# MLP up-projection as a 2x2 block product in seven products, with smaller blocks and the down-projections between the pairs

## Chip, cores and metric

One core of a Trainium2 chip runs the kernel in one launch. The metric is the device time in microseconds (us), the median of several runs of the same kernel.

## What is computed

One layer of a hybrid backbone for 640 tokens (512 latent, 128 context, `T = 640`) with a model width of 1024. The change touches only the gated MLP at the layer's end:

```python
h2 = rms_norm(x, n2) * (1 + sc2) + sh2
u_val, u_gate = jnp.split(dw_conv(h2 @ w_up, f_conv), 2, axis=-1)
x = x + gt2 * ((jax.nn.silu(u_gate) * u_val) @ w_dn)
```

`w_up` is 1024 x 5632 (2816 value columns, then 2816 gate columns), `w_dn` is 2816 x 1024, and `dw_conv` is a width-3 convolution along the tokens, done apart for the latent and the context tokens. Everything is float32.

## The kernel before, in words

Activations lie transposed in SBUF: 128 channels on the partitions, 640 tokens along a row. So `h2` is eight tiles of 128 channels (`KT = 8`), and the 2816 MLP channels are 22 tiles (`NF = 22`), each with a value tile (`uv`) and a gate tile (`ug`).

Each float32 product is made of three products in a shorter format (float32r). Every operand is split into a high part (a rounding cast on ScalarE) and a low part (the rest, a subtraction on VectorE), and TensorE sums high x high, low x high and high x low. For weights `w_split` does this (lines L142 and L143) from a staging buffer `raw` that `w_load` (L135) fills by a DMA on SP's queue. The `ring` holds three `raw` buffers and two each of `wh` and `wl`. `plan` is the list of all weight tiles in the order of use. `W(key)` takes the next one, and issues the load two entries ahead and the split one entry ahead, at a higher priority than the code around it.

`gemm_b` (L297) runs one tile of weights, 8 tiles deep for an up, over the 640 tokens in two halves of 320 (`HALF`): 8 x 3 x 2 = 48 matmuls of 320 columns. Its result stands in a `gtile` of two PSUM banks, and the pool `psg` has two such tiles, used in turn. A gemm can start only when the gemm before the last has been read out.

The MLP runs in four blocks of 6, 6, 5 and 5 channel tiles (`FBLK`). `ffn_up(b)` makes the value and gate tile of each channel tile, then `conv` (L438 on ScalarE, four operations of L440 on VectorE), SiLU (L1579), the product of the two (L1580), and a split into the high and low `ac` tiles (L330, L331). `ffn_down(b)` runs eight downs, one for each output tile `nt`, over the block's `ac` tiles (36 or 30 matmuls), and adds each to `x1[nt]` with two VectorE operations (L1589), one for the 512 latent columns and one for the 128 context columns. `ffn_up(b + 1)` stands ahead of `ffn_down(b)`. The first gemms of block 0 (`up_early`) start before the norm's scale is known.

The framework's scheduler takes the code and its priorities and sets the order in which each engine gets its instructions; that order is then fixed, and every engine runs its own strictly in turn.

Of the kernel before, what the change touches and what calls it, by code (L numbers as in the profile page):

```python
# [58 lines left out]
def hybrid_step(ctx: ExitStack, tc: tile.TileContext, a: dict, o: list):  # L59
# [27 lines left out]
    def body(ps):  # L87
        return ps[:, OFF:OFF + T]
# [110 lines left out]
    for nt in range(8):  # L199
        plan_cols(("wo", nt), w_out, nt * P)  # L200
    FBLK = [6, 6, 5, 5]
    fst = [0, 6, 12, 17]

    def plan_up(b):
        for f in range(fst[b], fst[b] + FBLK[b]):
            plan_cols(("uv", f), w_up, f * P)
            plan_cols(("ug", f), w_up, DFF + f * P)

    def plan_down(b):
        for nt in range(8):  # L210
            plan_cols(("wd", b, nt), w_dn_, nt * P, FBLK[b], P, fst[b])

    plan_up(0)
    for b in range(4):
        if b < 3:
            plan_up(b + 1)
        plan_down(b)

    pidx = {g[0]: i for i, g in enumerate(plan)}
    loaded, split = {}, {}  # L220
    LOOK_L, LOOK_S = 2, 1
    used = [0]

    def W(key):
        i = pidx[key]
        assert i == used[0], (key, i, used[0])
        used[0] += 1
        with tc.high_priority() if i else nullcontext():
            for j in range(i, min(i + LOOK_L + 1, len(plan))):
                if j not in loaded:  # L230
                    loaded[j] = w_load(*plan[j][1:])
                if j <= i + LOOK_S and j not in split:
                    split[j] = w_split(loaded[j], *plan[j][2:])
        return split[i]
# [1248 lines left out]
    gx = {}  # L1483

    def actile():
        return ep.tile([P, T + 2], F32R, tag="ac", bufs=24, name=nm("ac"))

    for nt in range(8):
        ps = gtile()
        if nt < 7:  # L1490
            x_load(nt + 1)
        gemm_b(ps, W(("wo", nt)), lambda k: mgH[:, k, :], lambda k: mgL[:, k, :], KT)
        x1[nt] = x()
        tr_chunks(xns.pop(nt).rearrange("p c x -> p (c x)"),
                  lambda c0, n, v, nt=nt: S.copy(x1[nt][:, c0 * P:(c0 + n) * P], v.rearrange("p c x -> p (c x)")))
# [3 lines left out]
        g, gh, gl = gx[nt] = [actile() for _ in range(3)]  # L1499
        for r, (c0, c1) in enumerate(((0, TS), (TS, T))):  # L1500
            S.activation(out=g[:, c0:c1].bitcast(F32), in_=x1[nt][:, c0:c1], func=AF.Copy, scale=A2[:, nt, r:r + 1])
        V.tensor_copy(g[:, T:].bitcast(F32), modc[:, 24 + nt, :])
        split_x(g.bitcast(F32), gh, gl)
        if nt == 0:
            S.activation(out=sacc, in_=x1[nt], func=AF.Square)
        else:
            sq = ep.tile([P, T], F32, tag="sq", bufs=2, name=nm("sq"))
            S.activation(out=sq, in_=x1[nt], func=AF.Square)
            (V if nt == 7 else G).tensor_tensor(out=sacc, in0=sacc, in1=sq, op=ALU.add)

    early = {}
# [25 lines left out]
    dg = ep.tile([P, T], F32, name="dg")
    rst = ep.tile([P, T], F32, name="rst")
    for c0, n in ((0, 4), (4, 1)):
# [3 lines left out]
        PE.matmul(out=pb[:, :n * P], lhsT=ones, rhs=dg[:, c0 * P:(c0 + n) * P], start=True, stop=True)  # L1543
        V.tensor_copy(rst[:, c0 * P:(c0 + n) * P], pb[:, :n * P])
    for _ in ug0:
        pass
    up_scale("uv", 0)
    up_scale("ug", 0)
    for _ in up_early("uv", 1):
        pass  # L1550
    h2H = actp.tile([P, KT, T], F32R, tag="aH", name="h2H")
    h2L = actp.tile([P, KT, T], F32R, tag="aL", name="h2L")
    for k in range(KT):
        g = gx[k][0][:, :T].bitcast(F32)
# [11 lines left out]
    def ffn_up(b, order):
        for f in order:
            ys = {}

            for key, f2 in sorted((("uv", f), ("ug", NF + f)), key=lambda i: (i[0], f) in early):  # L1570
                y = ys[key] = ep.tile([P, T], F32, tag="fy", bufs=4, name=nm("fy"))
                if (key, f) in early:
                    src = early[key, f]
                else:
                    ps = gtile()
                    gemm_b(ps, W((key, f)), lambda k: h2H[:, k, :], lambda k: h2L[:, k, :], KT)
                    src = body(ps)
                conv(y, src, lambda tap, f2=f2: fcols[:, tap, f2:f2 + 1])
            S.activation(out=ys["ug"], in_=ys["ug"], func=AF.Silu)  # L1579
            V.tensor_mul(ys["uv"], ys["uv"], ys["ug"])  # L1580
            ac[f] = [actile()[:, :T] for _ in range(2)]
            split_x(ys["uv"], *ac[f])

    def ffn_down(b):
        for nt in range(8):
            ps = gtile()
            gemm_b(ps, W(("wd", b, nt)), lambda k: ac[fst[b] + k][0], lambda k: ac[fst[b] + k][1], FBLK[b])
            for r, (c0, c1) in enumerate(((0, TS), (TS, T))):
                V.scalar_tensor_tensor(out=x1[nt][:, c0:c1], in0=body(ps)[:, c0:c1], scalar=modc[:, 40 + nt, r:r + 1],  # L1589
                                       in1=x1[nt][:, c0:c1], op0=ALU.mult, op1=ALU.add)  # L1590
            if b == 3:
                yt = ep.tile([P, NCH, P], F32, tag="xn", bufs=2, name=nm("yt"))
                tr_chunks(x1[nt], lambda c0, n, v: S.copy(yt[:, c0:c0 + n, :], v))
                ns_ = slice(nt * P, (nt + 1) * P)
                SY.dma_start(out=y_s[0, :, ns_].rearrange("(c p) d -> p c d", p=P), in_=yt[:, 0:4, :])
                SY.dma_start(out=y_p[0, :, ns_], in_=yt[:, 4, :])
# [40 lines left out]
```

## Time and profile before

| | us |
|---|---|
| median of 3 runs | 1397.82 (1394.4 to 1398.26) |
| profiled execution, its own time | 1397.2 |
| its span, first to last instruction | 1395.4 |

The profile comes from the profiled execution, which is 0.6 us below the median and has 1.8 us outside its span. In it TensorE is busy 96% of the span, VectorE 56%, ScalarE 38% and GpSimd 12%. The MLP takes about the last third: the chain of work that ended last shows one unbroken piece of TensorE work from 953.5 to 1355.4 us, and then the last eight downs with their transposes and stores.

### The profile page before, as it was taken

The page shows a single profiled execution, that of the slowest core. Times are in us where ns is not written, and L with a number is a line of the kernel's source. Part 1 is how long each engine was busy: PE and PEld are TensorE (multiplying, and loading weights), DVE is VectorE, ACT ScalarE, POOL GpSimd, SP SyncE. Part 2 cuts the span into 40 slices and gives each one's busy share as a digit, 9 for nine tenths or more (in the row PEclk, how much of TensorE's full clock was granted, in tenths as well). Part 3 has the DMA queues.
Part 4 walks back from the last instruction along what each step waited for, and adds up shares of the span by engine and source line. Part 5 has one row for each costly group of instructions (what it writes and reads, how often), then busy time and mean ns, then how long its engine had stood idle before and what let it go on. Part 6 is the DMA issues. An engine that isn't in the chain of part 4 may idle for free.

```text
span 1395.4 us, 26764 instructions
## 1 busy us (share of the span) xinstructions
PE 1339.1 (96%) x11201; PEld 1273.1 (91%) x11201; DVE 777.4 (56%) x1629; ACT 523.5 (38%) x968; POOL 168.2 (12%) x188
## 2 busy tenths in 40 slices
PE   5999999998989899999999998998999999999998
PEld 4899999898878798999998898998999999999998
DVE  3675876775788753334343335567555445535532
ACT  4543334422575432333333424554333223213312
POOL 1011122202223310102120022100000000000000
PEclk9999999998989999999999999999999999999999
DMA  9623331222012153434344534322222232132123
GB/s 273 169 61 86 98 78 41 56 76 64 24 32 55 40 105 94 111 94 112 102 120 144 149 89 140 99 76 61 76 76 65 73 91 69 58 97 70 54 85 86
DMA packets 198731, 123.79 MB, mean 89 GB/s; under 512 B 20341, under 2 KB 192147, under 8 KB 198611
## 3 DMA queue, kind: packets, MB, share of 16 engines
q1 hardware_dynamic: 198227, 121.76, 31.9%
q8 instruction: 88, 1.44, 0.4%
q10 hardware_dynamic: 384, 0.33, 0.1%
q14 instruction: 32, 0.26, 0.1%
HBM read 115.51 MB, written 6.55 MB: 87 GB/s over the span
## 4 chain that ended last, share of the span: by engine, by line
PE 74%; DVE 6%; ACT 4%; POOL 3%; issue 2%; DMA 0%; SPq 0%; ACTq 0%; DVEq 0%; POOLq 0%
PE g L297 60%; PE g L318 2%; PE s L545 1%; PE s L345 1%; PE s L1371 1%; DVE wl L143 1%; PE s L1359 1%; POOL ssn L267 1%; PE m L1321 1%; DVE stmp L903 1%; DVE Y L905 1%; POOL xa L1233 1%; POOL xb L1233 1%; PE m L1023 1%; PE m L715 1%
## 5 line engine op out<-in xcount | busy, mean ns | idle before, releaser
L142 ACT CAST wh<-raw 128x1024 fp32r<-128x1024 f32 (+3 forms) x172 | 161.4, 939 | 472.5 <-PE g L297 386.5
L143 DVE TENSOR_TENSOR wl<-raw,wh 128x1024 fp32r<-128x1024 f32 (+3 forms) x172 | 187.5, 1091 | 235.5 <-ACT wh L142 223.8
L297 PE MATMUL g<-hH,wh 128*128 128x320 f32 x768 | 187.2, 323 | 3.2 <-DVE xb L653 1.6
L297 PE MATMUL g<-hL,wh 128*128 128x320 f32 x768 | 183.4, 318 | 0.6 <-DVE hL L393 0.6
L297 PE MATMUL g<-hH,wl 128*128 128x320 f32 x768 | 183.5, 317 | 0.0
L297 PE MATMUL g<-h2H,wh 128*128 128x320 f32 x656 | 150.5, 311 | 4.0 <-DVE fy L440 4.0
L297 PE MATMUL g<-ac,wh 128*128 128x320 f32 (+1 forms) x800 | 151.7, 310 | 0.0
L297 PE MATMUL g<-h2L,wh 128*128 128x320 f32 x656 | 150.6, 311 | 0.0
L297 PE MATMUL g<-h2H,wl 128*128 128x320 f32 x656 | 150.4, 311 | 0.0
L297 PEld LDWEIGHTS g<-hH,wh 128*128 128x128 f32 x768 | 129.5, 191 | 11.8 <-issue 4.3
L297 PEld LDWEIGHTS g<-hL,wh 128*128 128x128 f32 x768 | 130.9, 192 | 3.3 <-issue 1.8
L297 PEld LDWEIGHTS g<-hH,wl 128*128 128x128 f32 x768 | 131.4, 192 | 2.3 <-issue 1.9
L297 PEld LDWEIGHTS g<-ac,wh 128*128 128x128 f32 x800 | 125.5, 188 | 0.2 <-issue 0.2
L297 PEld LDWEIGHTS g<-h2H,wh 128*128 128x128 f32 x656 | 110.7, 189 | 4.3 <-issue 4.3
L297 PEld LDWEIGHTS g<-h2H,wl 128*128 128x128 f32 x656 | 110.5, 189 | 0.0
L297 PEld LDWEIGHTS g<-h2L,wh 128*128 128x128 f32 x656 | 110.5, 189 | 0.0
L318 PE MATMUL g<-wh,hH 128*128 128x256 f32 x320 | 95.2, 297 | 3.4 <-DVE xb L653 3.4
L318 PE MATMUL g<-wl,hH 128*128 128x256 f32 x320 | 94.9, 297 | 0.0
L318 PE MATMUL g<-wh,hL 128*128 128x256 f32 x320 | 94.5, 295 | 0.0
L297 PE MATMUL g<-ac,wl 128*128 128x320 f32 (+1 forms) x400 | 91.7, 310 | 0.0
L440 DVE SCALAR_TENSOR_TENSOR fy<-g,fcols,fy 128x127 f32<-128x127 f32 (+1 forms) x164 | 86.1, 546 | 2.6
L1589 DVE SCALAR_TENSOR_TENSOR xa<-g,modc,xa 128x512 f32<-128x512 f32 x64 | 34.5, 548 | 89.2 <-PE g L297 89.2
(551 smaller groups left out, 2271.2 us busy)
## 6 DMA issues: line engine op xcount, KB each, us to landing
raw<-in_w_in_dram SPq DMA_DIRECT2D x64, 512.0 KB
raw<-in_w_up_dram SPq DMA_DIRECT2D x44, 512.0 KB
wada<-in_w_ada_dram SPq DMA_DIRECT2D x32, 512.0 KB
wat<-in_w_ada_dram SPq DMA_DIRECT2D x16, 512.0 KB
raw<-in_w_branch_dram SPq DMA_DIRECT2D x24, 256.0 KB
raw<-in_w_down_dram SPq DMA_DIRECT2D x16, 384.0 KB
raw<-in_w_down_dram SPq DMA_DIRECT2D x16, 320.0 KB
raw<-in_w_out_dram SPq DMA_DIRECT2D x8, 512.0 KB
```

The costliest lines, as they stand in the source:

```text
L142: S.copy(wh[:, :m], raw[:, :m])
L143: V.tensor_sub(wl[:, :m], raw[:, :m], wh[:, :m].bitcast(F32))
L267: G.tensor_tensor(out=out, in0=out, in1=mh.broadcast_to([P, n]), op=ALU.pow)
L297: PE.matmul(out=ps[:, OFF + c0:OFF + c1], lhsT=ww[:, k, :], rhs=xx(k)[:, c0:c1], start=(k == 0 and i == 0), stop=(k == kt - 1 and i == 2))
L318: PE.matmul(out=ps[b][:, o:o + GRP], lhsT=xx[:, 4 * kh + k, cs], rhs=ww[:, k, :], start=(kh == 0 and c % 2 == 0 and k == 0 and i == 0), st ...
L345: PE.matmul(out=pa[32 * g:32 * g + 32, :w], lhsT=csil[:, k, :], rhs=t[g], start=start, stop=stop)
L440: V.scalar_tensor_tensor(out=y[:, o0:o1], in0=src[:, i0:i0 + o1 - o0], scalar=w3(t), in1=y[:, o0:o1], op0=ALU.mult, op1=ALU.add)
L545: PE.transpose(pt[:, i * P:(i + 1) * P], src[:, (c0 + i) * P:(c0 + i + 1) * P], ident)
L715: PE.matmul(out=pv[b * w:(b + 1) * w, c, :], lhsT=K[r, c * P + b * w:c * P + (b + 1) * w], rhs=Q[r, c * P + qb * w:c * P + (qb + 1) * w], ...
L903: V.tensor_tensor(out=tv, in0=Uw[w, 0:k, k:k + 1].broadcast_to([64 + NB, k, m]), in1=Y[w, k:k + 1, k + 1:32].broadcast_to([64 + NB, k, m]) ...
L1233: G.tensor_tensor(out=out, in0=acc, in1=t, op=ALU.add)
L1589: V.scalar_tensor_tensor(out=x1[nt][:, c0:c1], in0=body(ps)[:, c0:c1], scalar=modc[:, 40 + nt, r:r + 1], in1=x1[nt][:, c0:c1], op0=ALU.mul ...
```

## The change

Blocks 1 to 5 are new: 22 tiles stand in six blocks of 4, 4, 4, 4, 3 and 3. Block 0 is made as before. From tile 4 on (18 tiles), `up_pair(f)` makes the value and the gate tile at once. Weights and activations are read as 2x2 matrices: the rows are value and gate, the inner index is the two halves of the 1024 channels (`kh`), the columns are the two token halves L and R. Seven products of 12 matmuls (4 channel tiles, three products each) take the place of eight (84 matmuls for a pair, 96 before). Four of the left factors and four of the right are sums or differences of blocks.

- Weights: four `plan` entries for a pair, named q0 to q3 here. `st_load` fetches the blocks. For q1 and q2 a second DMA on GpSimd's queue adds a block of `w_up` to what the first has landed (L250, `accum_op`). `st_sums` makes two more sums on VectorE (L258, L260). q0 to q2 are 1024 wide, q3 is 512.
- Activations: `sums_h2` makes, once, four sums and differences of `h2` for each of four channel tiles and splits them into the `hs` tiles.
- Results: X and Y are the two banks of one `gtile`, Z is an `stile` (one bank). X, Y and Z are each read between two products and added to again, so `up_pair` copies or combines parts in SBUF (`u1`, `u2`): two copies on ScalarE (L1689, L1699), five 320-column operations on VectorE. `conv` then reads `u1` and `u2` from SBUF.
- Downs: those of block b - 1 follow the pairs of block b, two after each pair (2, 3 and 3 in the blocks of three). There are 48 instead of 32, over 4 or 3 tiles (24 or 18 matmuls). Their weights have their own buffers (`rawd`, `whd`, `wld`, two each).

```diff
+    def st_load(f, j):
+        raw = st_raw[f, j] = ring.tile([P, 1024], F32, tag="raw", bufs=RAWB, name=nm("raw"))
...
+        SY.dma_start(out=lo, in_=part(*((0, 0), (1, 0), (0, 0), (1, 1))[j]))
+        if j in (1, 2):
+            G.dma_start(out=lo, in_=part(1, 2 - j), accum_op=ALU.add)
+        if j == 1:
+            SY.dma_start(out=hi, in_=part(0, 1))
+        return raw
+
+    def st_sums(f, j):
+
+        if j == 0:
+            V.tensor_add(st_raw[f, 0][:, 512:], st_raw[f, 0][:, :512], st_raw[f, 1][:, :512])
+        elif j == 2:
+            V.tensor_add(st_raw[f, 2][:, 512:], st_raw[f, 0][:, 512:], st_raw[f, 1][:, 512:])
...
+    def up_pair(f):
+
+        ps = gtile()
+        X, Y, Z = ps[:, :HALF], ps[:, 512:512 + HALF], stile()[:, :HALF]
...
+        w = W(("st", f, 0))
+        prod(X, w, 0, lambda j, k: hH2[j][:, k, L], True, False)
+        with tc.high_priority():
+            S.copy(u2[:, L], X)
+        prod(Y, w, 1, lambda j, k: hs[k, 1][j][:, R], True, False)
+        with tc.high_priority():
+            V.tensor_sub(u1[:, R], u2[:, L], Y)
+        w = W(("st", f, 1))
+        prod(Z, w, 0, lambda j, k: hs[k, 0][j][:, L], True, False)
+        with tc.high_priority():
+            V.tensor_add(u2[:, R], u2[:, L], Z)
+        prod(X, w, 1, lambda j, k: hH2[j][:, 4 + k, L], False, True)
+        with tc.high_priority():
+            S.copy(u1[:, L], X)
+        w = W(("st", f, 2))
+        prod(Y, w, 0, lambda j, k: hs[k, 0][j][:, R], False, False)
+        with tc.high_priority():
+            V.tensor_sub(u2[:, R], Y, u2[:, R])
+        prod(Z, w, 1, lambda j, k: hH2[j][:, 4 + k, R], False, True)
+        with tc.high_priority():
+            V.tensor_add(u1[:, R], u1[:, R], Z)
+        w = W(("st", f, 3))
+        prod(Y, w, 0, lambda j, k: hs[k, 1][j][:, L], False, True)
+        with tc.high_priority():
+            V.tensor_sub(u2[:, L], Y, u2[:, L])
...
-    ffn_up(0, (1, 2, 0, 3, 4, 5))
-    for b in range(4):
-        if b < 3:
-            ffn_up(b + 1, range(fst[b + 1], fst[b + 1] + FBLK[b + 1]))
-        ffn_down(b)
+    up_tile(1)
+    up_tile(2)
+    sums_h2(0)
+    sums_h2(1)
+    up_tile(0)
+    up_tile(3)
+    sums_h2(2)
+    sums_h2(3)
...
+    for b in range(1, NB_F):
+        for i in range(FBLK[b]):
+            up_pair(fst[b] + i)
+            for nt in downs(b, i):
+                down(b - 1, nt)
+    for nt in range(8):
+        down(NB_F - 1, nt)
```

How the scheduler then orders the instructions shows at three places. The first is TensorE at the start of a gemm that needs a PSUM tile. Before, at a down in the middle of a block (`g` is the down's PSUM tile, `ac` the gated activations, `wh` and `wl` its split weights; what an instruction waits for stands in brackets):

```order
L297 MATMUL g_1537_12821<-ac_1439_11772,wh_1534_12777 128x320 x2
L297 MATMUL g_1537_12821<-ac_1440_11773,wh_1534_12777 128x320 x2
L297 MATMUL g_1537_12821<-ac_1439_11772,wl_1535_12778 128x320 x2
L297 MATMUL g_1541_12866<-ac_1379_11132,wh_1538_12822 128x320 [waits DVE_49,PE_49,Activation_49]
L297 MATMUL g_1541_12866<-ac_1379_11132,wh_1538_12822 128x320
```

Now, at the start of a pair in the middle of a block (`s` is Z, `g` is X and Y, `r` are the `hs` tiles):

```order
L1681 MATMUL s_1442_12211<-r12_9538,wh_1444_12215 128x320
L1681 MATMUL s_1442_12211<-r13_9539,wh_1444_12215 128x320
L1681 MATMUL s_1442_12211<-r12_9538,wl_1445_12216 128x320
L1681 MATMUL g_1441_12210<-h2H_10355,wh_1439_12180 128x320 [waits DVE_49,PE_49]
L1681 MATMUL g_1441_12210<-h2L_10356,wh_1439_12180 128x320
L1681 MATMUL g_1441_12210<-h2H_10355,wl_1440_12181 128x320
```

Z's first product now stands ahead of X, and X waits for a VectorE instruction: the second addition (128 columns) of the first of the two downs ahead, whose PSUM tile X takes over. From X on the order in a pair is X (12 matmuls), 6 of a down, Y (12), 5 of that down, X again (12), 7 of Z, Y (12), 5 of Z, Y (12), the last 13 of that down, 24 of the second down, and the next pair's Z (12).

The second place is VectorE over the downs behind a pair. Before (`xa` is `x1[nt]`):

```order
L1589 SCALAR_TENSOR_TENSOR xa7_489<-g_1537_12821,modc_252,xa7_489 128x512
L143 TENSOR_TENSOR wl_1543_12868<-raw_1540_12826,wh_1542_12867 128x768
L1589 SCALAR_TENSOR_TENSOR xa7_489<-g_1537_12821,modc_252,xa7_489 128x128
L1589 SCALAR_TENSOR_TENSOR xa6_488<-g_1541_12866,modc_252,xa6_488 128x512
L143 TENSOR_TENSOR wl_1547_12913<-raw_1544_12871,wh_1546_12912 128x768
```

Now, the last 12 rows up to the addition for which X above waits (`t` are `u1`, `u2` and the convolution's results; ahead of these rows stand the last combination of the pair, L1710, then L260, one L489 of 511 columns and one L150 of 1024):

```order
L150 TENSOR_TENSOR wld_1454_12313<-rawd_1449_12278,whd_1453_12312 128x512
L150 TENSOR_TENSOR wl_1445_12216<-raw_1438_12175,wh_1444_12215 128x1024
L489 SCALAR_TENSOR_TENSOR t0_9519<-t2_9521,fcols_242,t0_9519 128x511
L489 SCALAR_TENSOR_TENSOR t0_9519<-t2_9521,fcols_242,t0_9519 128x127
L489 SCALAR_TENSOR_TENSOR t4_9523<-t3_9522,fcols_242,t4_9523 128x511
L150 TENSOR_TENSOR wld_1458_12347<-rawd_1452_12310,whd_1457_12346 128x512
L489 SCALAR_TENSOR_TENSOR t0_9519<-t2_9521,fcols_242,t0_9519 128x127
L489 SCALAR_TENSOR_TENSOR t4_9523<-t3_9522,fcols_242,t4_9523 128x511
L489 SCALAR_TENSOR_TENSOR t4_9523<-t3_9522,fcols_242,t4_9523 128x127
L1722 SCALAR_TENSOR_TENSOR xa5_487<-g_1433_12141,modc_252,xa5_487 128x512
L489 SCALAR_TENSOR_TENSOR t4_9523<-t3_9522,fcols_242,t4_9523 128x127
L1722 SCALAR_TENSOR_TENSOR xa5_487<-g_1433_12141,modc_252,xa5_487 128x128
```

A down's additions stood by themselves, with one weight split between them; now both convolutions and four weight splits of the pair stand ahead of them.

The third place is GpSimd's queue in the MLP. Before, its last rows were the sums of squares and one small power (`rs2`), and nothing came behind them:

```order
L1509 TENSOR_TENSOR sacc_9519<-sacc_9519,sq_1244_9838 128x640 [waits Activation_49,Pool_49]
L1509 TENSOR_TENSOR sacc_9519<-sacc_9519,sq_1255_9918 128x640 [waits Activation_49,Pool_49]
L1509 TENSOR_TENSOR sacc_9519<-sacc_9519,sq_1266_9998 128x640 [waits Activation_49,Pool_49]
L1509 TENSOR_TENSOR sacc_9519<-sacc_9519,sq_1277_10078 128x640 [waits Activation_49,Pool_49]
L267 TENSOR_TENSOR rs2_10219<-rs2_10219,mh_153 128x5 [waits DMAHW6_49,DVE_49]
```

Now 36 adding DMAs follow, two for a pair, here those of two pairs and the first of a third (q1, q2, q1, q2, q1):

```order
L250 DMA raw_1438_12175<-in_w_up_dram 128x4x128 [waits DMAHW1_49,DMASW5_49,DVE_49]
L250 DMA raw_1443_12212<-in_w_up_dram 128x4x128 [waits DMAHW3_49,DMAHW0_49,DMAHW5_49,DMASW2_49,DVE_49]
L250 DMA raw_1460_12377<-in_w_up_dram 128x4x128 [waits DMAHW0_49,DMASW7_49,DVE_49]
L250 DMA raw_1465_12414<-in_w_up_dram 128x4x128 [waits DMAHW4_49,DMAHW2_49,DMAHW7_49,DMASW4_49,DVE_49]
L250 DMA raw_1482_12579<-in_w_up_dram 128x4x128 [waits DMAHW7_49,DMASW1_49,DVE_49]
```

Each waits for the load on SP's queue that fills the same buffer, and that load in turn waits until VectorE has split the buffer's last content: q1's of the next pair takes over the buffer of q2.

## Rows read from the trace of the kernel before

**Rows 1.** The page's busy times by engine, whole span

```profile
PE 1339.1 (96%) x11201; PEld 1273.1 (91%) x11201; DVE 777.4 (56%) x1629; ACT 523.5 (38%) x968; POOL 168.2 (12%) x188
```

**Rows 2.** Busy time by stretch: engines with instruction counts, granted clock, DMA share, GB/s

```profile
1100.00:1200.00 100.00, 100.00 (x684) 100.00 (x684) 49.22 (x74) 27.61 (x33) 0.00 (x0) 1.00 0.26 77
```

**Rows 3.** The chain that ended last, in order of time: start, us, what

```profile
858.71 7.04 PE g L297 x48
...
953.52 401.88 PE g L297 x2725
```

**Rows 4.** Groups by shape, 955 to 1355 us: busy us, mean ns, idle before

```profile
L297 PE MATMUL g<-h2H,wl 128*128 128x320 f32 x624 | 143.1, 311 | 0.0
...
L440 DVE SCALAR_TENSOR_TENSOR fy<-g,fcols,fy 128x511 f32<-128x511 f32 x79 | 59.0, 747 | 1.3
...
L142 ACT CAST wh<-raw 128x1024 fp32r<-128x1024 f32 x37 | 38.9, 1050 | 118.1 <-PE g L297 118.1
...
L1589 DVE SCALAR_TENSOR_TENSOR xa<-g,modc,xa 128x512 f32<-128x512 f32 x25 | 18.8, 751 | 65.4 <-PE g L297 65.4
...
L330 ACT CAST ac<-fy 128x640 fp32r<-128x640 f32 x22 | 16.0, 726 | 16.3 <-DVE fy L1580 16.3
...
L1589 DVE SCALAR_TENSOR_TENSOR xa<-g,modc,xa 128x128 f32<-128x128 f32 x24 | 8.3, 345 | 0.0
...
L440 DVE SCALAR_TENSOR_TENSOR fy<-early,fcols,fy 128x511 f32<-128x511 f32 x4 | 3.0, 743 | 0.0
...
L440 DVE SCALAR_TENSOR_TENSOR fy<-early,fcols,fy 128x127 f32<-128x127 f32 x4 | 1.4, 342 | 0.0
```

**Rows 5.** VectorE's instructions in time, a dense stretch: start, us, line, operation

```profile
970.91 1.23 DVE L143 TENSOR_TENSOR wl<-raw,wh 128x1024 fp32r<-128x1024 f32 x1
972.05 0.82 DVE L331 TENSOR_TENSOR ac<-fy,ac 128x640 fp32r<-128x640 f32 x1
972.79 0.34 DVE L440 SCALAR_TENSOR_TENSOR fy<-early,fcols,fy 128x127 f32<-128x127 f32 x1
973.05 0.74 DVE L440 SCALAR_TENSOR_TENSOR fy<-g,fcols,fy 128x511 f32<-128x511 f32 x1
973.71 0.34 DVE L440 SCALAR_TENSOR_TENSOR fy<-early,fcols,fy 128x127 f32<-128x127 f32 x1
```

**Rows 6.** A 384 KB load: its issue on SP, then stretches with GB/s last

```profile
1101.97 0.37 SPq L135 DMA_DIRECT2D raw<-in_w_down_dram  x1
...
1102.50:1103.00 0.50, 0.50 (x5) 0.50 (x5) 0.00 (x0) 0.00 (x0) 0.00 (x0) 1.00 0.00 0
1103.00:1103.50 0.50, 0.50 (x6) 0.50 (x4) 0.00 (x0) 0.00 (x0) 0.00 (x0) 1.00 0.63 184
...
1104.50:1105.00 0.50, 0.50 (x6) 0.50 (x5) 0.00 (x0) 0.00 (x0) 0.00 (x0) 1.00 0.31 91
```

**Rows 7.** A 256 KB load behind others: issue, and the cast that waited

```profile
802.30 0.39 SPq L135 DMA_DIRECT2D raw<-in_w_branch_dram  x1
...
808.15 0.62 ACT L142 CAST wh<-raw 128x512 fp32r<-128x512 f32 x1 [5.86 <-DMA raw<-in_w_branch_dram]
```

**Rows 8.** The page's DMA queues: packets, MB, share

```profile
q1 hardware_dynamic: 198227, 121.76, 31.9%
```

**Rows 9.** Two waits of TensorE in time, and stretches around them

```profile
953.52 0.87 PE L297 MATMUL g<-h2H,wh 128*128 128x320 f32 x2 [4.04 <-DVE fy L440]
...
953.50:956.00 2.50, 2.48 (x9) 2.50 (x10) 2.45 (x6) 1.97 (x2) 0.00 (x0) 0.50 0.47 141
953.50:960.50 7.00, 6.98 (x32) 7.00 (x33) 3.88 (x8) 2.70 (x3) 0.00 (x0) 0.64 0.17 50
...
469.65 0.77 PE L1132 MATMUL s<-ident,xc 128*128 128x128 f32 x5 [2.68 <-DVE xc L1121]
...
470.40:477.20 6.80, 6.08 (x100) 5.31 (x99) 5.32 (x10) 2.60 (x6) 1.01 (x1) 0.50 0.05 12
```

More of the change, by code (lines that the diff above doesn't have):

```diff
@@ L230, in W @@
                 if j not in loaded:
-                    loaded[j] = w_load(*plan[j][1:])
-                if j <= i + LOOK_S and j not in split:
-                    split[j] = w_split(loaded[j], *plan[j][2:])
+                    loaded[j] = load_of(j)
+            for j in range(i, min(i + LOOK_S + 1, len(plan))):
+                if j not in split:
+                    split[j] = split_of(j)
         return split[i]
@@ L1536, in hybrid_step @@
         next(ug0)
[L1537 to L1538 removed]
+    dg = ft()
+    rst = ft()
     for c0, n in ((0, 4), (4, 1)):
@@ L1559, in hybrid_step @@
                                    in1=h2H[:, k, c0:c1].bitcast(F32), op0=ALU.add, op1=ALU.subtract)
     up_scale("uv", 1)
+    fslots.append(rst)
     ac = {}
[L1566 to L1587, printed above, removed]
-            for r, (c0, c1) in enumerate(((0, TS), (TS, T))):
[L1589 to L1596, printed above, removed]
@@ new lines, in up_pair, with prod @@
+    def up_pair(f):
+        ps = gtile()
+        X, Y, Z = ps[:, :HALF], ps[:, 512:512 + HALF], stile()[:, :HALF]
+        def prod(out, w, kh, xx, start, stop):
+            for k in range(4):
+                for i, (ww, hl_) in enumerate(((w[0], 0), (w[0], 1), (w[1], 0))):
+                    PE.matmul(out=out, lhsT=ww[:, 4 * kh + k, :], rhs=xx(hl_, k), start=start and k == 0 and i == 0,
+                              stop=stop and k == 3 and i == 2, skip_group_check=True)
+        hH2 = h2H, h2L
+        u1, u2 = ft(), ft()
+        w = W(("st", f, 0))
[23 more added lines that the diff above has]
+            V.tensor_sub(u2[:, L], Y, u2[:, L])
+        ys = [ft() for _ in range(2)]
+        for y, u, f2 in zip(ys, (u1, u2), (f, NF + f)):
+            conv(y, u, lambda tap, f2=f2: fcols[:, tap, f2:f2 + 1])
+        fslots.extend((u1, u2))
+        gated(f, *ys)
+        fslots.extend(ys)
@@ new lines, in down @@
+    def down(b, nt):
+        ps = gtile()
+        gemm_b(ps, W(("wd", b, nt)), lambda k: ac[fst[b] + k][0], lambda k: ac[fst[b] + k][1], FBLK[b])
+        for r, (c0, c1) in enumerate(((0, TS), (TS, T))):
+            V.scalar_tensor_tensor(out=x1[nt][:, c0:c1], in0=body(ps)[:, c0:c1], scalar=modc[:, 40 + nt, r:r + 1],
+                                   in1=x1[nt][:, c0:c1], op0=ALU.mult, op1=ALU.add)
+        if nt == 7:
+            for k in range(FBLK[b]):
+                slots.extend(ac.pop(fst[b] + k))
+        if b == NB_F - 1:
+            yt_ = ft()
+            yt = chunks(yt_)
+            tr_chunks(x1[nt], lambda c0, n, v: S.copy(yt[:, c0:c0 + n, :], v))
+            ns_ = slice(nt * P, (nt + 1) * P)
+            SY.dma_start(out=y_s[0, :, ns_].rearrange("(c p) d -> p c d", p=P), in_=yt[:, 0:4, :])
+            SY.dma_start(out=y_p[0, :, ns_], in_=yt[:, 4, :])
+            fslots.append(yt_)
```

145 lines of the change are left out of this document (108 added, 37 removed).

## The prediction

> **What bounds the kernel now.** I read the busy times first: TensorE works 96% of the span, the other engines far less [rows 1]. That is a mean, so the next view is the stretches: in the middle of the MLP TensorE is busy all 100 us, at the full granted clock, with 684 matmuls, while VectorE works 49.2 us, ScalarE 27.6 and GpSimd nothing [rows 2]. The chain that ended last agrees: from 953.52 us on it is 401.88 us of L297 without a break [rows 3]. So the MLP costs what its matmuls cost. One gemm of 48 takes 7.04 us in the same chain, 0.1467 us a matmul [rows 3]. A matmul row is 0.311 us long [rows 4], since matmuls overlap; the pitch is the price, and the rest, 0.16 us, is what a reader waits at the end.
>
> **What is removed.** 18 pairs lose 12 matmuls each: 216 x 0.1467 = 31.7 us, all on the path. The downs' matmuls are the same in sum.
>
> **What is added, per pair.** TensorE's own work for a pair with two downs is 84 + 48 = 132 matmuls, 19.4 us. The question is whether VectorE still hides behind it. Its prices are pitches in a dense stretch, start to start [rows 5]: 1.14 us for 1024 columns, 0.74 for 640, 0.66 for a convolution step of 511, 0.26 for one of 127. By the line between the first two, 512 columns cost 0.61 and 320 cost 0.41. The convolution read PSUM and now reads SBUF; its rows from an SBUF tile (`early`) are as long, 743 and 342 ns against 747 for the long one from PSUM [rows 4]. A down's two additions are as long as the steps of a convolution, 751 and 345 ns [rows 4], so 0.66 and 0.26. One pair then costs VectorE 3 splits of 1024 (3.4), one of 512 (0.6), two sums of weights (1.2), five combinations (2.1), eight convolution steps (3.7), product and split (1.5), two splits for downs (1.2) and four additions (1.8): 15.5 us. That is 80% of 19.4, so as a share it fits.
>
> As a chain it does not. PSUM has two `gtile`s, and X of a pair takes over the tile of the first down ahead of it, so X waits for that down's second addition. In VectorE's queue this addition stands 15 instructions behind the last combination of the pair before (L1710), which itself can't start before that pair's last Y product has ended. The 15 are three of 512 columns (1.83), two splits of 1024 (2.28), four steps of 511 (2.64), four of 127 (1.04) and the addition's own two (0.92): 8.7 us. Now walk from X to the next X. X to the end of the last Y is 83 matmuls, 12.2 us. The second Y waits on the way for a ScalarE copy behind a cast: by the 1050 ns of 1024 columns and the 726 of 640 [rows 4], 0.62 + 0.46 and 0.2 for handing over, against seven matmuls of Z, 1.03: 0.3. Then 0.2 to VectorE, 0.4 for L1710, 8.7 for the 15, and 0.1 back to TensorE. The sum is 21.9 us, where TensorE alone needs 19.4: **X waits 2.5 us in each round**. There are 17 rounds between 18 pairs. Two of them have downs of 18 matmuls, which cover 1.8 us less, while two narrower splits take 0.25 off the chain: I count 3.8 us. So 15 x 2.5 + 2 x 3.8 = 45.1 us.
>
> **The adding DMAs.** In the same VectorE queue the sum L258, which needs the added block of the next pair's q1, stands just ahead of L1710. Counted from X: the first Y ends after 30 matmuls (4.4), the cast of q2 ends 0.2 + 1.05 later, its low part 1.23 after that (6.9), and only then is q1's buffer free. A load of 256 KB follows. A load of 384 KB was issued at 1101.97, moved nothing until about 1103.0 and ended before 1105.0 [rows 6], so 256 KB take about 1.1 + 1.1 + 0.3 = 2.5 us: 9.4. Then GpSimd's DMA. To hide, it must be done when L258 has to start, 0.6 ahead of the end of the last Y at 12.7: 12.1, which leaves 2.7 us. No row shows such a DMA; all the data went through other queues, nearly all of it through this one [rows 8]. From below it takes the 2.5 us of the plain load, late by nothing; from above the 5.9 us of a 256 KB load that stood in a queue [rows 7], late by 3.2. I take 3.9, nearer to [rows 6], where nothing stood ahead: the target must be read as well as written, so 512 KB at that speed, 2.2 us, with 1.1 ahead, 0.3 behind, and 0.3 for two plain loads beside it. That is 1.2 late, with 0.1 for waking GpSimd 1.3: 17 x 1.3 = 22 us. The Trainium skill's page "DMA: Bandwidth & Descriptors", section "Anatomy of one DMA — SWDGE (gpsimd) path", gives a fixed 2.0 us and the bytes at 436 GB/s for one issued from GpSimd, an estimate of 2.6 us here. By that price nothing is late, and the sum below would be 1419; no run here shows it yet.
>
> **The edges.** `sums_h2` adds 16 operations of 320 columns (6.6) and eight splits of 640 (5.9) to VectorE, 12.5 us, at the place where it already holds TensorE up, in the wait for L440 [rows 9]. The convolutions that free PSUM for the last gemms of block 0 stand between them in the queue. Between 0 and 12.5 I take half, 6. Behind the last pair, its tile must be ready for the final downs: from L1710 through convolution, additions, splits, SiLU, product and cast about 10.4 us of VectorE and ScalarE, against 46 + 12 matmuls, 8.5: 2. The other additions cost nothing: the eight final downs shrink to 18 matmuls (2.6 us) and five transposes, against 1.4 us of VectorE for each; ScalarE's casts and copies of a pair come to about 9 us by the same rows; the extra bytes are small beside a DMA share of 0.26 [rows 2].
>
> **Sum.** -31.7 + 45.1 + 22 + 6 + 2 = +43.4 us. The profiled execution took 1397.2, 0.6 below the median: 1440.6, and 1441 for the median. A fair measure of this kernel tells about 0.3%, 4 us, from no change. The forecast's own range is 1411 (adding DMA never late, edges at nothing) to 1480 (late by 3.2, the first edge in full).
>
> **Rivals.**
> - *TensorE hides it all: 1374.* If the way from the last Y to the addition were under the 49 matmuls between them (7.2 us, I count 9.4), X would not wait; what is left is -31.7 + 8. For it: the mean load of 80%. Against it: the order is fixed, and every price in the chain is a row of the same operation. Chance 0.10.
> - *Even: 1397.* The same wait at half its size, with the DMAs hidden: 17 x 1.3 + 8 = 30 against 31.7. It needs a chain shorter by 1.2 us, 13%. Chance 0.05.
> - *The clock falls in each round: 1480.* After a wait of 4.04 us at 953.5 the granted clock was 0.50, the level of 1.2 GHz, for 2.5 us and more, and the 7.00 us from there held 32 matmuls, not 48: 2.3 us lost [rows 9]. The clock was also 0.50 behind a wait of 2.68 us in a stretch of small matmuls [rows 9]. Waits of 2.5 us or, in two pieces, 3.8 come close. 17 x 2.3 = 39 on top. Against it: between waits TensorE is dense, as it was not at 469 us. Chance 0.14. The Trainium skill warns of this on "TensorE: Matmul & The Clock Gate", section "HAM oscillation — how this bites in real kernels": a wait in every round of a loop can put the array back to the lower clock each time. The rows at 953.5 us agree for one wait.
> - *The adding DMA takes about 9 us: 1528.* Late by 6.4 instead of 1.3, 17 x 5.1 more. For it: nothing in this trace shows what GpSimd needs to write out 512 pieces of 512 bytes. Chance 0.09.
>
> **How the numbers follow.** The forecast has the remaining 0.62. Slower by over 0.3% are forecast, clock and slow DMA: 0.85; within, the even case: 0.05; faster: 0.10. The range of 1400 to 1482 leaves out the case of 1374 (0.10), the one of 1528 (0.09) and the lower half of the even one.
>
> **What would show it.** Right: 216 fewer matmuls; VectorE named as what X (L1681) waits for, 2 to 4 us in each round, with rounds of 22 to 24 us; VectorE at 65% to 75% of those rounds; L258 waiting for the adding DMA, its sum over all pairs about 20 us. Wrong: TensorE unbroken through the pairs (then the chain's prices are too high); the X wait small but a long wait for weights; a granted clock under 1 all through the pairs; or L258 never waiting, which takes out 22 us.

## The result and the profile after

The changed kernel takes 1498.34 us (median, 1494.1 to 1502.25), the kernel before 1397.82 (1394.4 to 1398.26): a ratio of 1.0724, with a 95% interval of 1.0685 to 1.0763. It is 100.5 us slower, where 43 had been forecast, and outside the range of 1400 to 1482. The profiled execution took 1501.0 us, its span 1498.4.

Busy times by engine, the answer to [rows 1]:

```profile
PE 1351.9 (90%) x10985; PEld 1263.0 (84%) x10985; DVE 893.0 (60%) x1863; ACT 581.1 (39%) x1080; POOL 217.5 (15%) x224
```

The 216 matmuls are gone (11201 to 10985), and yet TensorE is busy for 13 us longer: a part of its matmuls is slower. The same stretch as in [rows 2] shows how much was lost:

```profile
1100.00:1200.00 100.00, 81.49 (x505) 77.05 (x506) 62.28 (x106) 32.36 (x46) 10.29 (x8) 0.97 0.43 95
```

505 matmuls in 100 us, where there were 684. The waits from 950 us on, longest in total first (engine, what, who is waited for: us in total, times, longest), name the two places:

```profile
DVE raw L258 <- DMA raw<-in_w_up_dram: 68.3, 18, 5.0
...
PE g L1681 <- DVE xa L1722: 38.9, 14, 3.2
...
PE g L346 <- DVE t L1710: 31.7, 17, 2.7
...
PE g L346 <- DVE xa L1722: 10.5, 4, 3.2
```

X (L1681) waits for the addition of the first down, 2.8 us each time, in 14 of the 17 rounds. In the other three, which hold three downs, the third down (L346) waits for it instead. L258 waits for the adding DMA, 3.8 us each time, and TensorE gets 1.9 us of it as a wait for L1710. The chain that ended last, which had been one piece of TensorE work [rows 3], is now the same loop in each pair. One round of it, from X to the next X:

```profile
1141.95 3.13 PE g L1681 x12
1145.08 1.29 PE g L346 x6
1146.37 1.63 PE g L1681 x11
...
1148.02 1.06 ACT wh L149
...
1149.11 1.24 DVE wl L150
...
1150.36 3.09 DMA raw<-in_w_up_dram
...
1153.48 0.04 POOLq L250
1153.52 0.49 issue
1154.02 4.79 DMA raw<-in_w_up_dram
...
1158.83 0.04 DVE raw L258
1158.87 0.57 issue
1159.44 0.48 DVE t L1710
...
1168.35 0.27 DVE xa L1722
1168.62 0.14 issue
1168.76 1.38 PE g L1681 x7
```

X and Y, the split of q2 that frees a buffer (cast, then low part), the load of the next pair's q1 into it, the adding DMA, the sum L258, the combination L1710, VectorE's 15 instructions, and the next X: 26.8 us, all in series. From the first copy of X in one pair to that in the next, the 17 rounds took 464.5 us. Their 2286 matmuls at 0.1467 us would be 335.4, so **129 us** are lost in the rounds. The change in time is that, less 31.7 for the matmuls, and 3 us that remain for the edges.

X's first piece in that chain takes 3.13 us for 12 matmuls, not 1.76. The stretches around it (granted clock in the third column from the end):

```profile
1136.00:1139.00 3.00, 2.93 (x19) 2.44 (x17) 3.00 (x6) 0.67 (x2) 0.00 (x0) 1.00 0.65 184
1139.00:1142.00 3.00, 0.09 (x2) 0.08 (x1) 3.00 (x8) 0.36 (x1) 0.00 (x0) 1.00 0.56 166
1142.00:1145.00 3.00, 3.00 (x13) 3.00 (x14) 2.32 (x4) 1.11 (x2) 0.00 (x0) 0.57 0.00 0
1146.00:1156.00 10.00, 10.00 (x67) 9.58 (x66) 3.45 (x6) 2.83 (x4) 1.28 (x1) 1.00 0.28 80
```

TensorE stands still for 2.9 us, the granted clock falls to the level of 1.2 GHz for most of the next 3 us, and is back at 1.00 by 1146. The same happens behind 13 of the 15 waits for that addition of 2.8 to 3.2 us. Behind the other two, which end at 1116.74 and 1195.47 us, the clock stays at 1.00, and the rounds from there take 25.2 and 25.1 us where those beside them take 26.6 to 26.8: a fall costs some 1.5 us.

### The profile page after: what moved, and what is told of

Its sections match the earlier page's. It is cut to its first block, busy times and chain, and to the rows that moved or that the text cites. A ratio compares the mean times of both kernels' runs of the same rounds, so it can differ in the third digit from the quotient of the medians.

```text
span 1498.4 us, 27051 instructions
## 1 busy us (share of the span) xinstructions
PE 1351.9 (90%) x10985; PEld 1263.0 (84%) x10985; DVE 893.0 (60%) x1863; ACT 581.1 (39%) x1080; POOL 217.5 (15%) x224
## 4 chain that ended last, share of the span: by engine, by line
PE 45%; DVE 17%; DMA 10%; ACT 4%; issue 4%; POOL 3%; SPq 0%; ACTq 0%; POOLq 0%; DVEq 0%
PE g L346 30%; DMA raw<-in_w_up_dram 9%; PE g L1681 6%; DVE t L489 5%; DVE wl L150 4%; ACT wh L149 1%; DVE wld L150 1%; PE s L394 1%; PE s L594 1%; DVE xa L1722 1%; PE g L367 1%; PE s L1420 1%; PE s L1408 1%; PE m L1370 1%; DMA XT<-Xd 1%
## 5 line engine op out<-in xcount | busy, mean ns | idle before, releaser
L149 ACT CAST wh<-raw 128x1024 fp32r<-128x1024 f32 (+1 forms) x176 | 164.8, 945 | 381.8 <-PE g L346 168.6
L150 DVE TENSOR_TENSOR wl<-raw,wh 128x1024 fp32r<-128x1024 f32 (+1 forms) x176 | 192.8, 1098 | 168.5 <-ACT wh L149 158.9
L346 PE MATMUL g<-hH,wh 128*128 128x320 f32 x768 | 186.1, 321 | 3.0 <-DVE xb L702 1.5
L346 PE MATMUL g<-r,whd 128*128 128x320 f32 x704 | 149.7, 334 | 42.6 <-DVE t L1710 31.7
L346 PE MATMUL g<-hL,wh 128*128 128x320 f32 x768 | 183.7, 317 | 0.6 <-DVE hL L442 0.6
L346 PE MATMUL g<-hH,wl 128*128 128x320 f32 x768 | 182.5, 316 | 0.0
L346 PEld LDWEIGHTS g<-r,whd 128*128 128x128 f32 x704 | 121.8, 207 | 48.8 <-DVE t L1710 36.1
L346 PEld LDWEIGHTS g<-hH,wh 128*128 128x128 f32 x768 | 128.8, 191 | 11.3 <-issue 3.9
L346 PEld LDWEIGHTS g<-hL,wh 128*128 128x128 f32 x768 | 130.2, 190 | 3.4 <-issue 1.8
L346 PEld LDWEIGHTS g<-hH,wl 128*128 128x128 f32 x768 | 131.0, 191 | 2.2 <-issue 1.9
L250 POOL DMA_DIRECT2D raw<-in_w_up_dram x36 | 46.4, 1290 | 461.7 <-DMA raw<-in_w_up_dram 383.3
L1681 PE MATMUL g<-r,wh 128*128 128x320 f32 x432 | 101.3, 321 | 0.1
L346 PE MATMUL g<-r,wld 128*128 128x320 f32 x352 | 87.9, 327 | 0.0
L1681 PE MATMUL g<-h2H,wh 128*128 128x320 f32 x144 | 51.3, 356 | 40.4 <-DVE xa L1722 38.9
L489 DVE SCALAR_TENSOR_TENSOR t<-t,fcols,t 128x511 f32<-128x511 f32 (+1 forms) x156 | 78.4, 544 | 1.0 <-ACT t L487 1.0
L1681 PEld LDWEIGHTS g<-r,wh 128*128 128x128 f32 x432 | 72.4, 192 | 6.4 <-DVE t L1703 3.3
L346 PE MATMUL g<-oz,wh 128*128 128x320 f32 x384 | 73.8, 314 | 1.3 <-DVE xb L1281 1.2
L1681 PEld LDWEIGHTS g<-h2H,wh 128*128 128x128 f32 x144 | 29.8, 207 | 45.8 <-issue 42.2
```

The costliest lines, as they stand in the source:

```text
L250: G.dma_start(out=lo, in_=part(1, 2 - j), accum_op=ALU.add)
L346: PE.matmul(out=ps[:, OFF + c0:OFF + c1], lhsT=ww[:, k, :], rhs=xx(k)[:, c0:c1], start=(k == 0 and i == 0), stop=(k == kt - 1 and i == 2))
L489: V.scalar_tensor_tensor(out=y[:, o0:o1], in0=src[:, i0:i0 + o1 - o0], scalar=w3(t), in1=y[:, o0:o1], op0=ALU.mult, op1=ALU.add)
L1681: PE.matmul(out=out, lhsT=ww[:, 4 * kh + k, :], rhs=xx(hl_, k), start=start and k == 0 and i == 0, stop=stop and k == 3 and i == 2, skip_g ...
```

## The experiments

Theory: each round is this **loop**. Rivals: the DMAs cost by themselves, VectorE is full, X is slow for another reason than the clock. Ratios are to the kernel before in the same session, whose median there was 1393.0 to 1394.7 us.

### e1: X and Y in tiles of their own

```diff
-        ps = gtile()
-        X, Y, Z = ps[:, :HALF], ps[:, 512:512 + HALF], stile()[:, :HALF]
+        X, Y, Z = mtile()[:, :HALF], mtile()[:, :HALF], stile()[:, :HALF]
```

> X and Y of a pair each stand in a one-bank tile of their own (two unused banks of the other PSUM pool) instead of in the downs' tile, so that X no longer waits for a down's addition. Loop theory: a round is one loop in series, X to the split of q2 (8.4 us in the trace of the change), load of q1 and handing over (3.7), adding DMA (4.8), the sum L258 (0.6), L1710 and the VectorE chain to the addition that frees X's tile (9.3), 26.8 in all. With its own tile X needs only its weights, which are split 2 to 4 us behind L1710 instead of 9.3, and the way from X to the split of q2 shrinks to about 6: 18 to 19 us, less than the 19.4 that TensorE needs. So no wait of X, the granted clock at 1.0, 1375 to 1390 us. Rival, the DMAs alone: the round goes on waiting for the adding DMA and only the 2.9 us before X go: 1498 - 17 x 2.9 = 1449. Rival, VectorE is full: the wait moves to another place and the time stays within 10 us of 1498.

Measured: 1425.81 us, ratio 1.0214 (1.0182 to 1.0245), rounds mostly of 21 to 23 us.

```profile
DVE raw L258 <- DMA raw<-in_w_up_dram: 71.1, 18, 5.0
...
PE m L1680 <- ACT t L1688: 15.2, 10, 1.7
...
PE m L1680 <- DVE wl L150: 7.0, 10, 1.1
```

Two thirds of the slowdown are gone, more than the rival "the DMAs alone" allows, less than the loop theory gave. X waits for no addition any more, but L258 goes on waiting 4.0 us in each pair, and VectorE's queue stands behind it. TensorE now waits in smaller pieces for copies and splits that come late.

### e2 and e3: q1's buffer free a round earlier

```diff
-        raw = st_raw[f, j] = ring.tile([P, 1024], F32, tag="raw", bufs=RAWB, name=nm("raw"))
+        raw = st_raw[f, j] = (ring.tile([P, 1024], F32, tag="raw", bufs=RAWB, name=nm("raw")) if j < 3 else
+                              mlp["ep"].tile([P, 512], F32, tag="rawd", bufs=2, name=nm("rawd")))
...
```

> q3 is staged in the narrow ring of the downs' weights, so that q1 of the next pair takes over the buffer of its own predecessor (free a round earlier) and not that of q2. PSUM as in the change. Loop theory: load and adding DMA leave the loop, L258 waits for nothing; what is left is X to the last Y (12.5 us), L1710 and the VectorE instructions behind it; of the 15 ahead of the addition about 12 are left, 6.4 us: 19.7 us a round, so X waits 0 to 0.5 us and the clock stays up: 1375 to 1395 us. Rival, the chain of VectorE with the PSUM tile is what counts and not the DMAs: the wait for L258 goes, the wait of X of about 2.8 us stays and the clock still falls behind it: 1498 - 17 x 2.5 = 1455.

> Both edits. Loop theory: no loop is left that is near 19.4 us, TensorE runs the pairs without a break at full clock: 1397.2 - 31.7 + 0 to 12 for the sums of the activations = 1366 to 1378 us, a few us under either edit alone. Rival, the cost of the change lies in VectorE's and the DMAs' load and not in the order: above 1400 us.

Measured: e2 1463.84 us, ratio 1.0490 (1.0452 to 1.0528), rounds mostly of 23.8 to 26; e3 (with e1's edit) 1419.17 us, ratio 1.0156 (1.0118 to 1.0194). The wait that should have gone, in e2 and e3:

```profile
DVE raw L259 <- DMA raw<-in_w_up_dram: 61.7, 18, 4.6
```

```profile
DVE raw L259 <- DMA raw<-in_w_up_dram: 58.4, 18, 4.6
```

A miss for the theory's numbers: the loop closed again elsewhere. With the earlier buffer the scheduler also moved the sum (L259 here) up in VectorE's queue, to the additions of the downs, so it still meets a DMA on its way: q1's load waits for the split of the q1 before it, which stands well behind that sum in the same queue (in one round of e2 the sum began at 1180.37 and that split at 1194.74). These two runs don't tell whether the lateness or the mere presence of the DMAs costs. e5 and e6 take both away, e10 only shortens the DMAs. The mean split of 1024 columns takes VectorE 1.22 us in the rounds of the change, of e5 and of e10, so the traces show no price of their presence there.

### e4: useless matmuls in the wait

```diff
+        spare = mtile()[:, :HALF]
+        for i in range(16):
+            PE.matmul(out=spare, lhsT=h2H[:, i % 8, :P], rhs=h2L[:, i % 8, L], start=True, stop=True)
```

> Nothing of the change is undone. 16 useless matmuls of 320 columns for each pair go to a spare PSUM bank, ahead of X where TensorE waits for the addition. They are 18 x 16 x 0.1467 = 42 us of more work for TensorE. Clock theory: X's 12 matmuls take 3.1 us at the granted clock of 0.5 because TensorE stood still for 2.9 us; with the wait filled they take 1.8 and the round, which is bound by the loop, gets 1.4 to 1.9 us shorter: 1466 to 1475 us, faster with more work. Rival, X is slow for another reason (its weights, the port, the transfers beside it): X stays at 3 us, the time stays within 5 us of 1498 or rises.

Measured: 1481.75 us, ratio 1.0606 (1.0569 to 1.0643), against 1.0724 without. 42 us of work more, and 16.5 us less time (1.2% of 1398). Rounds went from about 26.3 to 24.9 us. The stretches around an X here:

```profile
1160.00:1163.00 3.00, 2.93 (x20) 2.68 (x19) 3.00 (x5) 0.95 (x2) 0.00 (x0) 1.00 0.59 173
1163.00:1166.00 3.00, 2.81 (x20) 2.54 (x18) 3.00 (x8) 0.08 (x1) 0.00 (x0) 1.00 0.60 175
1166.00:1169.00 3.00, 2.77 (x19) 2.75 (x19) 2.47 (x5) 1.80 (x3) 0.00 (x0) 1.00 0.03 6
```

The clock stays at 1.00 through X, which takes 2.0 us, and VectorE's way from the last combination to X is as long as in the change (9.3 us). So X was slow because TensorE had stood still: it takes 3.1 us in the change, 2.0 here.

### e5 and e6: without the adding DMAs

Both leave the second block out of the sums of q1 and q2; e6 has e1's tiles as well.

```diff
-        if j in (1, 2):
-            G.dma_start(out=lo, in_=part(1, 2 - j), accum_op=ALU.add)
```

> The two adding DMAs of each pair are left out (so the second block is missing from the sums of q1 and q2); loads, sums on VectorE, splits and matmuls stay. X and Y stand in the downs' PSUM tile as in the change. Loop theory: L258 no longer waits, and VectorE's order puts the split of q0 and the sum for q2 ahead of the last combination; about 7.0 us of VectorE are left behind it up to the addition that X waits for, so X to X is 12.5 + 0.2 + 0.5 + 7.0 = 20.2 us, with a wait of X under 1 us: rounds of 20 to 21 us, 1385 to 1410 us. Rival, the sum of the terms as forecast (22 us for the DMAs, the rest for X's wait, and the clock): the wait of X stays at 2.5 us and the clock still falls: 1498 - 17 x 3.3 = 1442.

> The adding DMAs left out as in e5, and X and Y in one-bank tiles of their own as in e1. Loop theory: both things that hold TensorE up in a round are gone, rounds of 19.4 to 19.8 us, granted clock 1.0: 1370 to 1382 us, which is what fewer matmuls alone are worth. Rival, splits and copies in VectorE's and ScalarE's fixed order hold the seven products up in any case: rounds of 21 us or more, 1400 us or more.

Measured: e5 1411.44 us, ratio 1.0137 (1.0106 to 1.0167), rounds of 21.0 us; e6 1373.78 us, ratio 0.9868 (0.9840 to 0.9897), rounds of 19.3 us. The waits of X in e5, and the stretch of [rows 2] in e6:

```profile
PE g L1679 <- DVE xa L1720: 10.1, 14, 2.1
```

```profile
1100.00:1200.00 100.00, 100.00 (x685) 100.00 (x684) 83.11 (x143) 43.78 (x61) 0.00 (x0) 1.00 0.33 96
```

e6 came as the loop theory had it. e5 lies a little over its range, with the rounds and the wait of X (0.7 us each time) that were expected. With the DMAs and the shared PSUM tile out of the way TensorE runs the pairs without a break, at the rate of before, beside a VectorE that is busy 83%. VectorE is not full; the order and the links held TensorE up. Of the change's 7.2%, cutting the DMAs takes 5.9 points (e5), and the tile 2.7 more (e5 to e6). In the other order the tile takes 5.1 (e1) and the DMAs 3.5 more (e1 to e6). The two lie on one loop, so neither number is a price of its own.

### e10: copies instead of additions, same queue

```diff
-            G.dma_start(out=lo, in_=part(1, 2 - j), accum_op=ALU.add)
+            G.dma_start(out=lo, in_=part(1, 2 - j))
```

> The change with one word less: GpSimd's DMAs only copy (the second block replaces the first instead of being added, so the sums are left out). Same queue, same bytes from HBM, same waits. If it is the adding that makes such a DMA take 4.8 us, a copy takes about the 3.1 us of a plain load from SP's queue, the loop of the round is 1.7 us shorter and the time 1498 - 17 x 1.7 = 1469 or, with the clock falling less often, down to 1455. If it is GpSimd's queue that is slow, the copy takes 4.3 us or more and the time stays within 8 us of 1498.

Measured: 1468.31 us, ratio 1.0538 (1.0510 to 1.0565). GpSimd's DMAs on the page (count, KB each, us from issue to landing) and their queue (packets, MB, share), first of the change, then of e10:

```profile
raw<-in_w_up_dram POOLq DMA_DIRECT2D x36, 256.0 KB, 4.8
...
q0 software_dynamic: 19008, 9.44, 5.2%
```

```profile
raw<-in_w_up_dram POOLq DMA_DIRECT2D x36, 256.0 KB, 3.4
...
q0 software_dynamic: 2880, 9.44, 2.3%
```

```profile
PE g L1681 <- DVE xa L1722: 39.6, 14, 2.9
...
PE g L346 <- DVE t L1710: 9.7, 17, 2.3
```

The adding is what makes it slow: 528 packets for each DMA where a copy has 80, and 1.4 us more until it lands. What goes is the wait for L1710 (31.7 to 9.7 us); X's wait (38.9 to 39.6) stays, since it hangs on VectorE's chain. But the clock behind it mostly stays up. One X in e10, and the stretch from it on:

```profile
1137.63 0.38 PE L1681 MATMUL g<-h2H,wh 128*128 128x320 f32 x1 [2.92 <-DVE xa L1722]
...
1137.60:1140.00 2.40, 2.37 (x16) 2.40 (x17) 1.87 (x4) 1.51 (x3) 0.00 (x0) 1.00 0.00 0
```

Of 16 such waits in e10, 3 are followed by a fall, where 13 of 15 were in the change. So a wait of 2.9 us alone does not bring the clock down. Here the round's other wait has shrunk from some 1.7 us to 0.2 to 0.5 in most rounds, but what decides is not shown. A round of 23.7 us is 3.1 shorter than one of 26.8: 1.5 for the DMA, and about as much for the clock. The loop theory's 1469 had only the DMA in it. That it is met is partly luck: the 17 rounds together are 37 us shorter, the time 30, since the long wait ahead of the pairs (4.04 us in [rows 9]) ends 6 us later in e10's trace than in the change's.

### e8 and e11: the regrouping alone

```diff
-            for j in range(4):
-                plan.append((("st", fst[b] + i, j), None, KT if j < 3 else 4, P))
+            f = fst[b] + i
+            plan_cols(("uv", f), w_up, f * P)
+            plan_cols(("ug", f), w_up, DFF + f * P)
...
-            up_pair(fst[b] + i)
+            up_tile(fst[b] + i)
```

> The other half of the change alone: blocks of 4, 4, 4, 4, 3 and 3 with the downs between the tiles, 48 downs, but each value and gate tile made in eight products by one gemm of 48 matmuls, as before; no sums of weights or activations. The matmuls are as many as before. Theory: the 32 additional additions of the 16 further downs, 16 us of VectorE, hide, and TensorE runs without a break: within 5 us of before, 1393 to 1402 us. Rival, the regrouping costs by itself (PSUM tiles used in turn, additions behind convolutions): 1410 us or more.

Measured: 1454.55 us, ratio 1.0437 (1.0405 to 1.0470). A miss: blocks of four with the downs between the tiles cost 61 us by themselves, with as many matmuls as before. TensorE's waits, and the chain from the end of a gate gemm to the second down:

```profile
PE g L347 <- DVE t L490: 34.4, 17, 4.1
```

```profile
1145.01 1.06 ACT wh L149
...
1146.10 1.23 DVE wl L150
1147.33 0.67 DVE t L490
...
1148.02 0.83 DVE t L490 x2
...
1148.94 0.74 DVE xa L1723
1149.69 0.60 DVE wld L150
1150.28 0.27 DVE t L490
1150.56 0.14 issue
1150.69 1.43 PE g L347 x8
```

The second down takes over the gate gemm's PSUM tile, whose last read (L490) ends 5.6 us after the gemm; the first down covers 3.5 us. The stretch of [rows 2]:

```profile
1100.00:1200.00 100.00, 90.46 (x593) 89.31 (x592) 48.75 (x80) 26.91 (x35) 0.00 (x0) 0.97 0.25 72
```

In e8's trace 18 waits for a PSUM tile, all but one of those shown and two for a down's addition, are 35 of the 62 us by which the span is longer, and the clock falls behind 8 of them. Another 10 us lie ahead of these rounds (the wait that ended at 953.52 [rows 9] ends at 963.10) and are not explained. e11 gives the downs one-bank tiles of their own:

```diff
-        ps = gtile()
+        pl, pr = mtile()[:, :HALF], mtile()[:, :HALF]
...
```

> As e8 (regrouped blocks, eight products), but each down writes two one-bank tiles of its own instead of the two-bank tile that it shares with the value and gate gemms; each down then takes three additions on VectorE instead of two. Theory: in e8 the second down of each tile waits 2.0 us for the convolution of the gate gemm, whose PSUM tile it takes over, because only the 3.5 us of the first down cover the 5.6 us from the end of the gate gemm to the last read of its tile. With tiles of their own the downs wait for nothing, the clock stays up, and the time is back within 6 us of before: 1388 to 1400 us. Rival, it is VectorE's and ScalarE's order (splits ahead of convolutions) that holds TensorE up: the wait moves to the next gemm and the time stays above 1430 us.

Measured: 1408.00 us, ratio 1.0098 (1.0060 to 1.0136).

```profile
1100.00:1200.00 100.00, 100.00 (x684) 100.00 (x683) 53.81 (x96) 29.21 (x38) 0.00 (x0) 0.95 0.27 79
```

684 matmuls, as many as before although the granted clock of this execution reads 0.95, and TensorE unbroken: the theory is right on the wait. It missed the last 1%, which lies outside the rounds. Of the 12.4 us by which the span is longer, 7 lie ahead of the rounds as in e8, again not explained, and 3 are waits of the last transposes for the downs' additions (4.1 us in seven waits, 0.9 in one before).

### e7 and e9: the same result without adding DMAs

The sums need no second load: all their terms are the four blocks of the pair. Each is loaded once, q3 with the downs' weights, X and Y as in e1. In e7 two additions on GpSimd take the place of the DMAs; e9 gives VectorE the two that are needed first:

```diff
-            G.dma_start(out=lo, in_=part(1, 2 - j), accum_op=ALU.add)
...
+            V.tensor_add(q2[:, :512], q0[:, :512], q1[:, :512])
+            V.tensor_add(q0[:, 512:], q2[:, :512], raw)
+            G.tensor_tensor(out=q1[:, :512], in0=q1[:, :512], in1=raw, op=ALU.add)
+            G.tensor_tensor(out=q2[:, 512:], in0=q0[:, 512:], in1=q1[:, 512:], op=ALU.add)
...
```

> The same result as the change without adding DMAs: each of the four blocks of a pair is loaded once, and the two sums that the DMAs made are two additions of 512 columns on GpSimd (q2 = first block + third block, then q1 = third block + fourth). q3 is staged with the downs' weights; X and Y in one-bank tiles of their own. An addition of 640 columns took GpSimd 2.4 us in this kernel, so 1.9 us each, behind the split of q2 that frees the buffer: ready at about 6 + 4 = 10 us after X, needed at about 12. Loop theory: rounds of 19.4 to 20 us, 1370 to 1390 us. Rival, GpSimd beside VectorE slows one of them or comes late: waits of VectorE for GpSimd, rounds of 21 to 22 us, 1400 to 1420 us.

> As e7, with the sums in another order, so that VectorE never waits for GpSimd: VectorE makes q2's first half (first + third block) and adds the fourth block to it for q0's second half; GpSimd makes only the two sums that are needed last (q1's first half, q2's second half). VectorE does as many additions of weights as in the change. Theory: in e7 the 2.1 us that VectorE waits for GpSimd in each round come back as TensorE's wait for L1710 (7.4 us in all) and rounds of 20.1 us; without them the rounds are 19.3 us as in e6, and the time is 1370 to 1380 us. Rival, what is left in e7 comes from VectorE's and GpSimd's work itself: rounds of 20 us again, 1384 to 1392 us.

Measured: e7 1388.54 us, ratio 0.9966 (0.9950 to 0.9981), rounds of 20.1 us; e9 1380.79 us, ratio **0.9903** (0.9882 to 0.9924), most rounds 19.3 us. e7's two waits, then e9's stretch:

```profile
DVE raw L263 <- POOL raw L257: 35.7, 17, 2.4
...
PE m L1688 <- DVE t L1710: 7.4, 13, 1.1
```

```profile
1100.00:1200.00 100.00, 100.00 (x685) 100.00 (x684) 87.42 (x140) 44.57 (x63) 16.78 (x10) 1.00 0.29 83
```

e9 is 1% faster than the kernel before, and no kernel that leaves nothing out was faster. In e7 GpSimd, off the path by its share, held VectorE up by 2.1 us a round only because VectorE's queue came to the sum before GpSimd had it. e9's median lies a little over its expectation; TensorE still waits where the downs come in threes (4.8 us in four waits).

## Why the prediction was wrong, step by step

- **-31.7 us for 216 matmuls: right.** e6 shows it as the rounds of 19.3 us that 132 matmuls should take.
- **X waits 2.5 us in each round: right.** 2.8 measured, and still 2.8 in e10, where the DMA is shorter. From the start of L1710 to the next X there are 9.3 us in the chain; 0.4 + 8.7 + 0.1 had been counted. The number belongs to VectorE's order in the change: in e5, where the split of q0 and the sum for q2 stand ahead of the last combination, it is 0.7. The rounds with three downs were counted as if they had two; there the third down waits instead of X, about as long.
- **The adding DMAs, "1.3 late, 17 x 1.3 = 22 us": the first step that failed, in its size.** Load and adding DMA were put at 2.5 + 0.1 + 3.9 = 6.5 us. In the chain they take 3.09 for the load, 0.57 until GpSimd's DMA begins, and 4.79 until it lands: 8.45, or 2.0 us more in each round (0.6 for the load, 0.5 until the start, 0.9 for the DMA), about 33 us in 17. The adding DMA lies within the bounds that were set for it (2.5 to 5.9 us), and the mechanism was the one named; the chosen value was too near to a plain load. The load and the 0.1 for waking GpSimd had been given no bounds. The Trainium skill's page "DMA: Bandwidth & Descriptors", section "Anatomy of one DMA — SWDGE (gpsimd) path", gives a fixed 2.0 us and the bytes at 436 GB/s, an estimate of 2.6 us. The measurement decides: 3.4 for the copy and 4.8 with the addition.
- **The clock, set aside as a rival of 0.14: the second step that failed.** From X's start to the end of q2's split 6.9 us were counted; 8.4 were measured, and nearly all of the 1.5 is X and what follows it at the lower clock. The rival's price was 2.3 a round. A fall cost some 1.5, and it came in most rounds. The argument against it, that TensorE is dense between waits, did not hold in the change, where TensorE waits twice in a round; e4 shows the cause, and e10 that the wait of X is not enough by itself. The Trainium skill's page "TensorE: Matmul & The Clock Gate", section "HAM oscillation — how this bites in real kernels", says that a wait in every round of a loop can put the array back to the lower clock each time. The granted clock of 0.57 behind a wait of 2.9 us in the rows above agrees; e10's 1.00 behind a wait as long shows that it need not be so.
- **The sum.** Round forecast: 6.9 + 6.5 + 9.8 = 23.2 us. Round measured: 8.4 + 8.45 + 9.9 = 26.8. Over all rounds 129 us were lost, not 67; for the edges 3 remain, not 8. The forecast treated the slow DMA and the clock as cases that exclude each other, each with its own time. They go together, for what is late makes TensorE wait, and behind its waits the clock mostly falls; the range held either, not both. The 2.0 and the 1.5 us are 59 of the 62 us that were missing in 17 rounds.
- **The rivals.** That TensorE hides all, 1374 us, is nearly what e6 reaches once the two links are cut (its ratio of 0.9868 would be 1379 here); the change as it stands has both. Of the signs listed ahead, X's wait and the matmul count came as said. Rounds of 22 to 24 us and 20 us for L258 did not (26 to 27 mostly, and 68), nor did VectorE at 65% to 75% of the rounds: it is busy for 61%, since the rounds are longer. The stretch of the rounds, with their granted clock:

```profile
981.20:1452.20 471.00, 390.24 (x2339) 369.33 (x2340) 289.49 (x486) 152.06 (x215) 43.66 (x34) 0.94 0.39 86
```

## What to carry to other kernels

When an order is fixed, look for the loop, not only for the busiest engine: a buffer or a PSUM tile that one kind of work takes over from another closes it, and every latency on it is paid in each round. Cut the link (a tile of its own, data that is already there) before making a step on it faster. And a wait in every round is priced with the clock that may fall behind it, as one case, not as two.

## What was not expected of the hardware

An adding DMA of 256 KB from GpSimd went as 528 packets, its copy as 80, and landed 1.4 us later (4.8 against 3.4). 16 useless matmuls in each round made the kernel 16.5 us faster, since they kept the granted clock at 1.00 in most rounds. And waits of the same 2.9 us were followed by the level of 1.2 GHz 13 times in 15 in the change, 3 times in 16 in e10.
